# x in two of five raw weight buffers, and eight k tiles through seven products in every second column block of FFN 2

## The chip, the cores and the metric

The kernel runs on one core of one Trainium2 chip. The metric is the time of one execution in microseconds of device time. Engines are named as in the profile: PE (matmul) with PEld (its weight loads), DVE (vector), ACT (scalar), POOL (GpSimd) and SP, whose queue issues most transfers.

## The reference

One encoder layer on x of 256 rows by 2048 columns, in f32. What matters here is the residual x and the two half FFNs:

```python
D_MODEL = 2048
SEQ = 256
D_FF = ((8 * D_MODEL // 3 + 255) // 256) * 256   # 5632

def swiglu(h, w_gate, w_up, w_down):
    return (jax.nn.silu(h @ w_gate) * (h @ w_up)) @ w_down
...
        x = x + 0.5 * swiglu(rms_norm(x, ffn1_norm[i]), ffn1_w_gate[i], ffn1_w_up[i], ffn1_w_down[i])
        h = rms_norm(x, mix_norm[i])
        proj = h @ w_in[i]
...
        x = x + mixed @ w_out[i]
        x = x + 0.5 * swiglu(rms_norm(x, ffn2_norm[i]), ffn2_w_gate[i], ffn2_w_up[i], ffn2_w_down[i])
        gate = jax.nn.sigmoid(rms_norm(x, ple_norm[i]) @ w_ple_gate[i])
...
        x = x + rms_norm(e, ple_post_norm[i])
```

Between the two FFNs stand a state space mixer and a stick-breaking attention, after them a gated embedding.

## The kernel before

Rows are in two tiles of 128 (`TT` = 2), columns in blocks of 512 (`NB`), k in tiles of 128. Every f32 operand of a large product is split into a high part of lower precision (`whi`, `nhi`: a cast on ACT, L168) and the rest (`wlo`, `nlo`: a subtraction on DVE, L171). A product is three matmuls of 128x128 by 512: high by high (L292), low by high (L293), high by low (L297).

Weights come as `raw` tiles of four k tiles by 512 columns (1 MB) through three buffers. A tile is split half by half (two k tiles) into four buffers of `whi` and `wlo`. A plain half is 12 matmuls: 2 k tiles, 2 row tiles, 3 products. FFN 1 and FFN 2 each run 11 column blocks (f = 0 to 10) of gate and up, turn each block's result through `mid` and DMAs into `hT`, and then run four column blocks of down over 44 k tiles.

In FFN 2, from f = 1 on, the first chunk of four k tiles of gate and up goes through seven products instead of eight (`gemm_seven`): with the gate and up tiles cut in halves along k, the weights b11, b21 (gate) and b12, b22 (up) are added on DVE (`sum`, L459: t1 = b11 + b12, t2 = t1 + b22, t4 = t2 + b21, t3 = b12 + b22) and split into `shi` and `slo`; the sums of the rows (`sum_forms`) are made once, while f = 0 runs. A product is 6 matmuls (L452, L453, L455), so the chunk takes 42 where plain halves take 48. The other three chunks of gate follow plainly, then those of up. `opened` and `gated` (L531 to L540) and the lines L545 and L547 close a block by adding the products' accumulators and gating; `turned` transposes it (L203).

The program is written in order and a scheduler lays the instructions out on each engine; `put_off(n, fn)` runs `fn` n steps (`step()`, one after each half or product or two) later. A tile of a pool waits for a free buffer of its tag, in the order of the program. The four `acc` accumulators and two double ones, `aux`, are PSUM.

The residual x stays in its own eight tiles (`xt`, 16 KB in each partition) all through: loaded in FFN 1's block 0 for the sums of squares, added to after down (L594) and after the output projection (L1339).

Of the kernel before, what the change touches and what calls it, by code (L numbers as in the profile page):

```python
# [9 lines left out]
F32 = mybir.dt.float32  # L10
# [6 lines left out]
P = 128  # L17
# [16 lines left out]
def layer_kernel(ctx: ExitStack, tc: tile.TileContext, a: dict, shapes: dict, out: bass.AP):  # L34
# [18 lines left out]
    xpool = ctx.enter_context(tc.tile_pool(name="xres", bufs=1))  # L53
# [86 lines left out]
    xt = [[xpool.tile([P, NB], F32, name=f"x_{t}_{n}") for n in range(ND)] for t in range(TT)]  # L140
# [96 lines left out]
    def first_quarters(w, xn):  # L237

        rest = com("h")
        raws = [wp.tile([P, 4, NB], F32, tag="raw", name=uid("raw"), bufs=3) for _ in range(2)]  # L240
# [37 lines left out]
    def weight_halves(w, k0, nk, n0, own=None):  # L278

        raw = wp.tile([P, 4, NB], F32, tag="raw", name=uid("raw"), bufs=3)  # L280
        src = w[k0 * P : (k0 + nk) * P, n0 : n0 + NB].rearrange("(j p) n -> p j n", p=P)
        nc.sync.dma_start(raw[:, :nk, :], src)
        return weight_split(raw, nk, own)
# [125 lines left out]
    def sum_forms(parts):  # L409
# [9 lines left out]
        for z, (x, y, op) in enumerate((  # L419
            (up[:, :, 1], down[:, :, 1], ALU.subtract), (s[:, 0], up[:, :, 0], ALU.subtract),  # L420
            (up[:, :, 0], up[:, :, 1], ALU.subtract), (down[:, :, 0], s[:, 1], ALU.add),
        )):
            nc.vector.tensor_tensor(out=s[:, z], in0=x, in1=y, op=op)
        both = halves("n")
        split(*both, sums.rearrange("p (z t) -> p z t", z=4))
        return both

    def gemm_seven(act, sums, ws, n0, nkt, pool, first, second):

        raws = []  # L430
        for w in ws:
            raw = wp.tile([P, 4, NB], F32, tag="raw", name=uid("raw"), bufs=3)
            nc.sync.dma_start(raw, w[: 4 * P, n0 : n0 + NB].rearrange("(j p) n -> p j n", p=P))
            raws.append(raw)
        b11, b21, b12, b22 = (raw[:, 2 * h : 2 * h + 2, :] for raw in raws for h in range(2))
        parts = act(0)

        def whole(k, t):
            return [[u[:, 2 * k + j, t * P : (t + 1) * P] for j in range(2)] for u in parts]

        def summed(z):
            return [[u[:, z, j * P : (j + 1) * P] for j in range(2)] for u in sums]

        def product(ps, left, src, own, stop):
            hi, lo = (
                (pool if own else wp).tile([P, 2, NB], F32R, tag=s, name=uid(s), bufs=3 if own else None)
                for s in (("shi", "slo") if own else ("whi", "wlo"))
            )
            split(hi, lo, src)
            lh, ll = left  # L450
            for j in range(2):
                nc.tensor.matmul(ps, lhsT=lh[j], rhs=hi[:, j], start=j == 0, stop=False)  # L452
                nc.tensor.matmul(ps, lhsT=ll[j], rhs=hi[:, j], start=False, stop=False)  # L453
            for j in range(2):
                nc.tensor.matmul(ps, lhsT=lh[j], rhs=lo[:, j], start=False, stop=stop and j == 1)  # L455

        def add(x, y):
            t = pool.tile([P, 2, NB], F32, tag="sum", name=uid("sum"), bufs=2)
            nc.vector.tensor_tensor(out=t, in0=x, in1=y, op=ALU.add)  # L459
# [23 lines left out]
        for w, banks, fresh in ((ws[0], [p2, p4], False), (ws[1], [p38[:, :NB], p38[:, NB:]], True)):  # L483
            for k0 in range(4, nkt, 4):
                part = act(k0 // 4)
                for half in list(weight_halves(w, k0, 4, n0)):
                    begin = k0 == 4 and half[0] == 0
                    end = k0 + 4 >= nkt and half[0] == 1
                    for t in range(TT):
                        gemm_half({t: banks[t]}, (part, half), (t,), fresh and t == 1 and begin, end)  # L490
                    step()
            if not fresh:
                put_off(0, second, p2, p4, p5)
        return p38

    def ffn(i, xn, nxt, bg=None):
# [23 lines left out]
        for f in range(NF):  # L520
# [5 lines left out]
            if sevens and f:  # L526
# [3 lines left out]
                def opened(p1, p67, g=gate_cols, u=up_cols):  # L530
                    nc.scalar.copy(g[0], p1)  # L531
                    nc.vector.tensor_tensor(out=u[0], in0=p67[:, :NB], in1=g[0], op=ALU.add)
                    nc.vector.tensor_tensor(out=u[1], in0=p67[:, NB:], in1=u[0], op=ALU.add)
# [1017 lines left out]
```

## Time and profile before

| | |
|---|---|
| runs | 1870.79, 1872.24, 1873.25 us; median 1872.24 |
| profiled execution | 1872.24 us, span 1870.4 us |
| TensorE clock granted | 1.0 throughout |
| matmuls | 9134 |
| DMA | 400.06 MB, mean 214 GB/s |

The stages, by what their lines do in the trace: FFN 1 gate and up to about 490 us, its down to 737, the mixers to 975, the output projection to 1056, FFN 2 gate and up to 1497, its down to 1737, then the embedding. Busy time in these stretches (us):

| stretch | PE | DVE | ACT | POOL |
|---|---|---|---|---|
| 0 to 490 | 487.85 | 314.56 | 223.46 | 23.23 |
| 490 to 737 | 247.00 | 174.38 | 144.98 | 2.33 |
| 737 to 975 | 234.66 | 162.37 | 150.90 | 19.20 |
| 975 to 1056 | 81.00 | 55.75 | 42.04 | 3.72 |
| 1056 to 1497 | 440.43 | 354.66 | 226.10 | 0.00 |
| 1497 to 1737 | 240.00 | 170.35 | 140.07 | 0.00 |
| 1737 to 1870 | 128.45 | 78.34 | 68.91 | 1.89 |

A busy PE is not a PE at its peak: matmuls are pipelined, so the starts of matmuls, not their lengths, tell the pace.

### The profile page before, as it was taken

The page shows a single profiled execution, that of the slowest core. Times are in us where ns is not written, and L with a number is a line of the kernel's source. Part 1 is how long each engine was busy: PE and PEld are TensorE (multiplying, and loading weights), DVE is VectorE, ACT ScalarE, POOL GpSimd, SP SyncE. Part 2 cuts the span into 40 slices and gives each one's busy share as a digit, 9 for nine tenths or more (in the row PEclk, how much of TensorE's full clock was granted, in tenths as well). Part 3 has the DMA queues.
Part 4 walks back from the last instruction along what each step waited for, and adds up shares of the span by engine and source line. Part 5 has one row for each costly group of instructions (what it writes and reads, how often), then busy time and mean ns, then how long its engine had stood idle before and what let it go on. Part 6 is the DMA issues. An engine that isn't in the chain of part 4 may idle for free.

```text
span 1870.4 us, 23938 instructions
## 1 busy us (share of the span) xinstructions
PE 1859.4 (99%) x9134; PEld 1536.3 (82%) x9134; DVE 1310.4 (70%) x1527; ACT 996.5 (53%) x1151; POOL 50.4 (3%) x84
## 2 busy tenths in 40 slices
PE   9999999999999999999999999999999999999998
PEld 7888888888888888878888888888888888888887
DVE  8867665455576776687567678778787866777655
ACT  7444444444456665456695555445454555666554
POOL 0011000000000000010020000000000000000000
PEclk9999999999999999999999999999999999999999
DMA  8788867766655666675645666575666675656563
GB/s 323 242 278 268 267 208 222 231 217 200 217 196 199 212 199 244 185 248 163 222 147 189 218 205 221 203 220 186 203 205 208 225 228 203 204 202 212 189 224 124
DMA packets 230387, 400.06 MB, mean 214 GB/s; under 512 B 26401, under 2 KB 50337, under 8 KB 229985
## 3 DMA queue, kind: packets, MB, share of 16 engines
q1 hardware_dynamic: 227824, 392.81, 63.7%
q0 software_dynamic: 1728, 4.33, 0.7%
q8 instruction: 71, 1.16, 0.3%
q10 hardware_dynamic: 720, 1.41, 0.2%
q14 instruction: 44, 0.35, 0.1%
HBM read 369.26 MB, written 9.83 MB: 203 GB/s over the span
## 4 chain that ended last, share of the span: by engine, by line
PE 92%; ACT 3%; DVE 2%; DMA 1%; SPq 1%; issue 1%; POOL 0%; DVEq 0%; ACTq 0%; POOLq 0%
PE acc L292 26%; PE acc L297 26%; PE acc L293 26%; PE aux L293 3%; PE aux L292 3%; PE aux L297 3%; ACT whi L168 1%; SPq L1061 1%; PE acc L455 1%; DMA raw<-in_w_in 1%; PE aux L452 1%; PE acc L452 1%; PE acc L453 1%; PE aux L455 1%; PE aux L453 1%
## 5 line engine op out<-in xcount | busy, mean ns | idle before, releaser
L171 DVE TENSOR_TENSOR wlo<-raw,whi 128x1024 fp32r<-128x1024 f32 x656 | 798.2, 1224 | 458.9 <-ACT whi L168 455.3
L168 ACT CAST whi<-raw 128x1024 fp32r<-128x1024 f32 x656 | 686.2, 1053 | 758.7 <-PE acc L293 607.9
L292 PE MATMUL acc<-whi,nhi 128*128 128x512 f32 x1408 | 551.0, 391 | 1.2 <-ACT whi L260 0.5
L293 PE MATMUL acc<-whi,nlo 128*128 128x512 f32 x1408 | 548.2, 389 | 0.0
L297 PE MATMUL acc<-wlo,nhi 128*128 128x512 f32 x1408 | 384.4, 389 | 0.0
L292 PE MATMUL acc<-whi,hhi 128*128 128x512 f32 x816 | 317.6, 389 | 0.0
L293 PE MATMUL acc<-whi,hlo 128*128 128x512 f32 x816 | 317.5, 389 | 0.0
L292 PEld LDWEIGHTS acc<-whi,nhi 128*128 128x128 f32 x1408 | 264.3, 188 | 58.3 <-ACT whi L168 1.7
L297 PEld LDWEIGHTS acc<-wlo,nhi 128*128 128x128 f32 x1408 | 264.2, 188 | 55.6 <-DVE wlo L171 0.4
L293 PEld LDWEIGHTS acc<-whi,nlo 128*128 128x128 f32 x1408 | 264.4, 188 | 54.0
L297 PE MATMUL acc<-wlo,hhi 128*128 128x512 f32 x816 | 221.0, 389 | 0.0
L297 PEld LDWEIGHTS acc<-wlo,hhi 128*128 128x128 f32 x816 | 152.8, 188 | 32.5 <-DVE wlo L171 0.9
L293 PEld LDWEIGHTS acc<-whi,hlo 128*128 128x128 f32 x816 | 153.2, 188 | 32.0
L292 PEld LDWEIGHTS acc<-whi,hhi 128*128 128x128 f32 x816 | 153.1, 188 | 31.8
L171 DVE TENSOR_TENSOR hlo<-hT,hhi 128x1024 fp32r<-128x1024 f32 x88 | 107.1, 1218 | 0.0
L168 ACT CAST hhi<-hT 128x1024 fp32r<-128x1024 f32 x88 | 91.8, 1044 | 0.5 <-PE acc L455 0.4
L292 PE MATMUL aux<-whi,nhi 128*128 128x512 f32 x160 | 62.2, 389 | 0.0
L293 PE MATMUL aux<-whi,nlo 128*128 128x512 f32 x160 | 62.2, 389 | 0.0
L297 PE MATMUL aux<-wlo,nhi 128*128 128x512 f32 x160 | 49.3, 389 | 0.0
L171 DVE TENSOR_TENSOR slo<-sum,shi 128x1024 fp32r<-128x1024 f32 x40 | 48.6, 1214 | 0.4 <-ACT shi L168 0.2
L168 ACT CAST shi<-sum 128x1024 fp32r<-128x1024 f32 x40 | 42.1, 1052 | 11.5 <-DVE sum L459 11.4
L297 PEld LDWEIGHTS aux<-wlo,nhi 128*128 128x128 f32 x160 | 30.0, 188 | 6.2
(312 smaller groups left out, 1314.5 us busy)
## 6 DMA issues: line engine op xcount, KB each, us to landing
raw<-in_ffn_w_up SPq DMA_DIRECT2D x88, 1024.0 KB, 5.9
raw<-in_ffn_w_down SPq DMA_DIRECT2D x88, 1024.0 KB, 5.0
raw<-in_ffn_w_gate SPq DMA_DIRECT2D x86, 1024.0 KB, 5.4
raw<-in_w_in SPq DMA_DIRECT2D x32, 1024.0 KB, 5.5
raw<-in_w_out SPq DMA_DIRECT2D x16, 1024.0 KB, 5.1
raw<-in_w_ple_gate SPq DMA_DIRECT2D x16, 1024.0 KB, 5.1
hT<-mid SPq DMA_DIRECT2D x160, 64.0 KB, 5.0
h<-mid SPq DMA_DIRECT2D x176, 32.0 KB, 3.4
```

The costliest lines, as they stand in the source:

```text
L168: copy = nc.scalar.copy(hi, src)
L171: nc.vector.tensor_tensor(out=lo, in0=src, in1=hi.bitcast(F32), op=ALU.subtract)
L292: nc.tensor.matmul(ps[t], lhsT=lh, rhs=hi[:, j, cols], start=start and j == 0, stop=False)
L293: nc.tensor.matmul(ps[t], lhsT=ll, rhs=hi[:, j, cols], start=False, stop=False)
L297: nc.tensor.matmul(ps[t], lhsT=lh, rhs=lo[:, j, cols], start=False, stop=stop and j == 1)
L452: nc.tensor.matmul(ps, lhsT=lh[j], rhs=hi[:, j], start=j == 0, stop=False)
L453: nc.tensor.matmul(ps, lhsT=ll[j], rhs=hi[:, j], start=False, stop=False)
L455: nc.tensor.matmul(ps, lhsT=lh[j], rhs=lo[:, j], start=False, stop=stop and j == 1)
L1061: nc.sync.dma_start(zt[0][p1 : p1 + HC, z], sv[p0 : p0 + HC, r % 2 * 2 + r // 2])
```

## The change

x gives up its own tiles. The raw weights get five buffers instead of three, and x lives in two of the five: while it is only needed for the sums of squares in FFN 1's block 0, from FFN 1's down to the start of FFN 2, and from FFN 2's down to the end. For the gate and up blocks in between it is given up: before each down stage `fetch_x` loads it again through POOL's queue, in FFN 1 from the input, in FFN 2 from a copy in DRAM (`scr_x`) that is written, also through POOL's queue, as the output projection finishes each column block.

In FFN 2, blocks f = 1, 3, 5, 7, 9 take a second chunk through seven products: chunk 0, then gate's chunks 2 and 3 plainly, then chunk 1 by seven products into the same accumulators, then up's chunks 2 and 3. Even blocks keep one such chunk. The products come in another order (1, 5, 6, 4, 7, 2, 3), and the row sums are made for two chunks, in the `sum` buffers instead of `h`. In the built order PE has 30 matmuls fewer (8610 matmul rows for 8640), DVE 41 instructions more, ACT 16 more, and POOL 24 transfers of 256 KB more.

```diff
-    xpool = ctx.enter_context(tc.tile_pool(name="xres", bufs=1))
...
-    xt = [[xpool.tile([P, NB], F32, name=f"x_{t}_{n}") for n in range(ND)] for t in range(TT)]
+    xt = [[], []]
+
+    def place_x():
+        for t in range(TT):
+            x = wp.tile([P, ND, NB], F32, tag="raw", name=uid("x"), bufs=5)
+            xt[t][:] = [x[:, n, :] for n in range(ND)]
+
+    def fetch_x(rows):
+        place_x()
+        for n in range(ND):
+            for t in range(TT):
+                nc.gpsimd.dma_start(xt[t][n], rows[t * P : (t + 1) * P, n * NB : (n + 1) * NB])
+
+    place_x()
+    scr_x = dramp.tile([T, D], F32, name="scr_x")
...
-        raw = wp.tile([P, 4, NB], F32, tag="raw", name=uid("raw"), bufs=3)
+        raw = wp.tile([P, 4, NB], F32, tag="raw", name=uid("raw"), bufs=5)
...
+    def whole_rows(pool, parts):
 
         hi, lo = parts
-        whole, sums = com("h"), com("h")
-        u = whole.rearrange("p (j t m) -> p j t m", j=4, t=TT)
+        u = pool.tile([P, 2, NB], F32, tag="sum", name=uid("whole"), bufs=2)
         nc.vector.tensor_tensor(
-            out=whole.rearrange("p (j t) -> p j t", j=4), in0=hi.bitcast(F32), in1=lo.bitcast(F32), op=ALU.add
+            out=u.rearrange("p j n -> p (j n)"), in0=hi.bitcast(F32).rearrange("p j t -> p (j t)"),
+            in1=lo.bitcast(F32).rearrange("p j t -> p (j t)"), op=ALU.add,
         )
-        s = sums.rearrange("p (z j m) -> p z j m", z=4, j=2)
-        up, down = u[:, :2], u[:, 2:]
+        return u.rearrange("p j n -> p (j n)").rearrange("p (j x b) -> p j x b", j=4, b=32)
...
+            (a21, a22, ALU.subtract), (s[:, 0], a11, ALU.subtract),
+            (a11, a21, ALU.subtract), (a12, s[:, 1], ALU.add),
...
-        p1, p2 = acc(), acc()
-        product(p1, whole(0, 0), b11, False, True)
-        product(p2, whole(1, 0), b21, False, False)
-        step()
-        t1 = add(b11, b12)
-        p5 = acc()
-        product(p5, summed(0), t1, True, True)
-        t2 = add(t1, b22)
-        p67 = aux()
-        product(p67[:, :NB], summed(1), t2, True, True)
-        step()
-        t4 = add(t2, b21)
-        p4 = acc()
-        product(p4, whole(1, 1), t4, True, False)
-        t3 = add(b12, b22)
-        product(p67[:, NB:], summed(2), t3, True, True)
-        step()
-        p38 = aux()
-        product(p38[:, :NB], summed(3), b22, False, False)
-        step()
-        put_off(0, first, p1, p67)
...
+        def chunk(self, kb, final=()):
+
+            raws = []
+            for w, n0 in self.ws:
+                raw = wp.tile([P, 4, NB], F32, tag="raw", name=uid("raw"), bufs=5)
+                nc.sync.dma_start(
+                    raw, w[4 * kb * P : 4 * (kb + 1) * P, n0 : n0 + NB].rearrange("(j p) n -> p j n", p=P)
+                )
+                raws.append(raw)
+            b11, b21, b12, b22 = (raw[:, 2 * h : 2 * h + 2, :] for raw in raws for h in range(2))
+            parts, sums = self.act(kb), self.sums(kb)
...
+            self.product(1, whole(0, 0), b11, False, final)
+            t1 = self.add(b11, b12)
+            self.product(5, summed(0), t1, True, final)
+            step()
+            t2 = self.add(t1, b22)
+            self.product(6, summed(1), t2, True, final)
+            t4 = self.add(t2, b21)
+            self.product(4, whole(1, 1), t4, True, final)
+            step()
+            t3 = self.add(b12, b22)
+            self.product(7, summed(2), t3, True, final)
+            self.product(2, whole(1, 0), b21, False, final)
+            step()
+            self.product(3, summed(3), b22, False, final)
...
+                s = Seven(xn, lambda kb: sums[kb], ((wg, f * NB), (wu, f * NB)), sevens)
+                if f % 2 == 0:
+                    s.chunk(0, shared)
+                    put_off(0, opened, s)
+                    s.column(0, (1, 2, 3), True)
+                    put_off(0, gated, s)
+                    s.column(1, (1, 2, 3), True)
+                else:
+                    s.chunk(0)
+                    s.column(0, (2, 3))
+                    s.chunk(1, (*shared, 2, 4))
+                    put_off(0, opened, s)
+                    put_off(0, gated, s)
+                    s.column(1, (2, 3), True)
+                nc.vector.tensor_tensor(out=hh, in0=s.banks[3.8], in1=hh, op=ALU.add)
...
-                sums = sum_forms(xn(0))
+                sums = [sum_forms(sevens, whole_rows(sevens, xn(kb))) for kb in range(2)]
...
+        fetch_x(a["x"][0] if bg else scr_x)
...
+            for t in range(TT):
+                nc.gpsimd.dma_start(scr_x[t * P : (t + 1) * P, n * NB : (n + 1) * NB], xt[t][n])
```

DVE, at the start of column block f = 3 (raw_9753 and raw_9755 are its first gate and up tiles, raw_9710 the last up tile of f = 2). Before:

```order
L171 TENSOR_TENSOR wlo_9713<-raw_9710,whi_9712 128x1024
L171 TENSOR_TENSOR wlo_9717<-raw_9710,whi_9716 128x1024
L171 TENSOR_TENSOR wlo_9760<-raw_9753,whi_9759 128x1024
L171 TENSOR_TENSOR wlo_9770<-raw_9753,whi_9769 128x1024
L459 TENSOR_TENSOR sum_9779<-raw_9753,raw_9755 128x1024
L459 TENSOR_TENSOR sum_9792<-sum_9779,raw_9755 128x1024
L171 TENSOR_TENSOR slo_9783<-sum_9779,shi_9782 128x1024
L171 TENSOR_TENSOR wlo_9835<-raw_9755,whi_9834 128x1024
L545 TENSOR_TENSOR h_9428<-aux_9509,h_9428 128x1024
L171 TENSOR_TENSOR slo_9796<-sum_9792,shi_9795 128x1024
L547 SCALAR_TENSOR_TENSOR h_9428<-h_9428,sm_8834,sg_9427 128x512 x2
L459 TENSOR_TENSOR sum_9805<-sum_9792,raw_9753 128x1024
```

And now (raw_9788 and raw_9790 are the gate and up tiles, raw_9745 the last up tile of f = 2):

```order
L184 TENSOR_TENSOR wlo_9748<-raw_9745,whi_9747 128x1024
L487 TENSOR_TENSOR sum_9803<-raw_9788,raw_9790 128x1024
L184 TENSOR_TENSOR wlo_9752<-raw_9745,whi_9751 128x1024
L184 TENSOR_TENSOR slo_9806<-sum_9803,shi_9805 128x1024
L487 TENSOR_TENSOR sum_9816<-sum_9803,raw_9790 128x1024
L184 TENSOR_TENSOR wlo_9793<-raw_9788,whi_9792 128x1024
L487 TENSOR_TENSOR sum_9829<-sum_9816,raw_9788 128x1024
L184 TENSOR_TENSOR slo_9819<-sum_9816,shi_9818 128x1024
L184 TENSOR_TENSOR wlo_9855<-raw_9788,whi_9854 128x1024
L184 TENSOR_TENSOR slo_9832<-sum_9829,shi_9831 128x1024
L487 TENSOR_TENSOR sum_9842<-raw_9790 128x1024
L184 TENSOR_TENSOR wlo_9869<-raw_9790,whi_9868 128x1024
```

The first sums now stand ahead of the last split of the block before, and the add that closes that block (L545, now L601) has moved behind the chunk's third weight split.

DVE, in the middle of the same block. Before, after the first chunk, where gate's second and third tiles (raw_9844 and raw_9881) are split plainly:

```order
L171 TENSOR_TENSOR wlo_9847<-raw_9844,whi_9846 128x1024
L171 TENSOR_TENSOR wlo_9851<-raw_9844,whi_9850 128x1024
L532 TENSOR_TENSOR h_9752<-aux_9794,sg_9751 128x512
L171 TENSOR_TENSOR wlo_9884<-raw_9881,whi_9883 128x1024
L533 TENSOR_TENSOR h_9752<-aux_9794,h_9752 128x512
L171 TENSOR_TENSOR wlo_9888<-raw_9881,whi_9887 128x1024
L171 TENSOR_TENSOR wlo_9918<-raw_9915,whi_9917 128x1024
L171 TENSOR_TENSOR wlo_9922<-raw_9915,whi_9921 128x1024
```

And now the second chunk's products, from the split of t1 (sum_9961) to the split of t3 (sum_9997), with raw_9947 and raw_9949 its gate and up tiles and raw_10029 the next up tile:

```order
L184 TENSOR_TENSOR slo_9964<-sum_9961,shi_9963 128x1024
L487 TENSOR_TENSOR sum_9973<-sum_9961,raw_9949 128x1024
L184 TENSOR_TENSOR wlo_9952<-raw_9947,whi_9951 128x1024
L487 TENSOR_TENSOR sum_9985<-sum_9973,raw_9947 128x1024
L184 TENSOR_TENSOR slo_9976<-sum_9973,shi_9975 128x1024
L184 TENSOR_TENSOR wlo_10010<-raw_9947,whi_10009 128x1024
L184 TENSOR_TENSOR slo_9988<-sum_9985,shi_9987 128x1024
L487 TENSOR_TENSOR sum_9997<-raw_9949 128x1024
L184 TENSOR_TENSOR wlo_10020<-raw_9949,whi_10019 128x1024
L184 TENSOR_TENSOR wlo_10032<-raw_10029,whi_10031 128x1024
L184 TENSOR_TENSOR wlo_10036<-raw_10029,whi_10035 128x1024
L184 TENSOR_TENSOR slo_10000<-sum_9997,shi_9999 128x1024
```

Where plain weight splits stood, sums and splits that depend on one another now stand.

SP's queue, the loads of the same block. Before:

```order
L433 DMA raw_9753<-in_ffn_w_gate 128x4x512
L433 DMA raw_9755<-in_ffn_w_up 128x4x512
L282 DMA raw_9844<-in_ffn_w_gate 128x4x512
L282 DMA raw_9881<-in_ffn_w_gate 128x4x512
L282 DMA raw_9915<-in_ffn_w_gate 128x4x512
L282 DMA raw_9949<-in_ffn_w_up 128x4x512
L282 DMA raw_9988<-in_ffn_w_up 128x4x512
L282 DMA raw_10022<-in_ffn_w_up 128x4x512
```

And now:

```order
L495 DMA raw_9788<-in_ffn_w_gate 128x4x512
L495 DMA raw_9790<-in_ffn_w_up 128x4x512
L295 DMA raw_9879<-in_ffn_w_gate 128x4x512
L295 DMA raw_9913<-in_ffn_w_gate 128x4x512
L495 DMA raw_9947<-in_ffn_w_gate 128x4x512
L495 DMA raw_9949<-in_ffn_w_up 128x4x512
L295 DMA raw_10029<-in_ffn_w_up 128x4x512
L295 DMA raw_10071<-in_ffn_w_up 128x4x512
```

One gate and one up tile of the plain stretch became the pair of the second chunk (the two rows L495 in the middle).

More of the change, by code (lines that the diff above doesn't have):

```diff
@@ L481, in gemm_seven, with whole, summed @@
[L481 to L488 removed]
+        def chunk(self, kb, final=()):
[8 more added lines that the diff above has]
+            parts, sums = self.act(kb), self.sums(kb)
+            def whole(k, t):
+                return [[u[:, 2 * k + j, t * P : (t + 1) * P] for j in range(2)] for u in parts]
+            def summed(z):
+                return [[u[:, z, j * P : (j + 1) * P] for j in range(2)] for u in sums]
+            self.product(1, whole(0, 0), b11, False, final)
[12 more added lines that the diff above has]
+            self.product(3, summed(3), b22, False, final)
+            step()
@@ L489, in gemm_seven, with column @@
+        def column(self, side, kbs, final=False):
+            zs = ((2, 4), (3, 8))[side]
+            w, n0 = self.ws[side]
+            for kb in kbs:
+                part = self.act(kb)
+                for half in list(weight_halves(w, 4 * kb, 4, n0)):
+                    end = final and kb == kbs[-1] and half[0] == 1
                     for t in range(TT):
-                        gemm_half({t: banks[t]}, (part, half), (t,), fresh and t == 1 and begin, end)
+                        ps = self.bank(zs[t])
+                        gemm_half({t: ps}, (part, half), (t,), self.begin(zs[t]), end)
```

80 lines of the change are left out of this document (44 added, 36 removed).

## The prediction

> **What bounds the kernel now.** I read the page's busy shares and chain first, then the TensorE rows of a calm stage, then FFN 2's gate and up stage by its timeline, groups and waits.
>
> ```profile
> PE 1859.4 (99%) x9134; PEld 1536.3 (82%) x9134; DVE 1310.4 (70%) x1527; ACT 996.5 (53%) x1151; POOL 50.4 (3%) x84
> PE 92%; ACT 3%; DVE 2%; DMA 1%; SPq 1%; issue 1%; POOL 0%; DVEq 0%; ACTq 0%; POOLq 0%
> ```
>
> PE is the bound: busy 99% of the span and 92% of the chain. But its mean of 389 ns per matmul is a latency, not a price. The timeline of the first down product gives the price:
>
> ```profile
> 524.89 1.07 PE L297 MATMUL acc<-wlo,hhi 128*128 128x512 f32 x4
> ...
> 527.61 1.07 PE L297 MATMUL acc<-wlo,hhi 128*128 128x512 f32 x4
> ```
>
> One half tile (12 matmuls) takes 527.61 - 524.89 = 2.72 us, so a matmul costs 2.72/12 = 0.2267 us. Next, the starts of five FFN 2 column blocks (f = 1 to 5), each the first matmul of its seven products:
>
> ```profile
> 1097.51 0.39 PE L452 MATMUL acc<-whi,hhi 128*128 128x512 f32 x1
> 1139.79 0.39 PE L452 MATMUL acc<-whi,hhi 128*128 128x512 f32 x1
> 1182.26 0.39 PE L452 MATMUL acc<-whi,hhi 128*128 128x512 f32 x1
> 1225.14 0.39 PE L452 MATMUL acc<-whi,hhi 128*128 128x512 f32 x1
> 1267.49 0.39 PE L452 MATMUL acc<-whi,hhi 128*128 128x512 f32 x1
> ```
>
> A block has 42 + 144 = 186 matmuls, 42.16 us at 0.2267. The blocks took 42.28, 42.47, 42.88 and 42.35: f = 3 loses 0.72 us, f = 4 only 0.19. So the stage runs within 2% of what PE can do, and the loss is in the odd block. Who makes PE wait there (first row), and what held the rest up, stands in the waits of 1066 to 1490 us, the last row being the load queue's:
>
> ```profile
> PEld aux L452 <- ACT shi L168: 2.7, 5, 0.6
> ACT whi L168 <- DMA raw<-in_ffn_w_gate: 20.3, 9, 5.1
> SPq L282 <- DVE sum L459: 138.4, 20, 14.5
> ```
>
> PE waits for the split of a sum; the sum is late because the loads wait (up to 14.5 us) for the DVE to let go of one of three raw buffers.
>
> **The change part by part.** *Fewer matmuls.* A chunk of four k tiles costs 48 matmuls for gate and up plainly, 42 by seven products. The change does a second chunk so in f = 1, 3, 5, 7, 9: 5 x 6 = 30 matmuls fewer, 30 x 0.2267 = 6.80 us, all on the path. [...]
>
> *More work for DVE.* Prices are from the groups of 1066 to 1450 us; the last row is a window, with the busy time of PE, PEld, DVE and ACT:
>
> ```profile
> L171 DVE TENSOR_TENSOR wlo<-raw,whi 128x1024 fp32r<-128x1024 f32 x134 | 162.6, 1221 | 77.2 <-ACT whi L168 76.9
> L171 DVE TENSOR_TENSOR slo<-sum,shi 128x1024 fp32r<-128x1024 f32 x36 | 43.7, 1214 | 0.4 <-ACT shi L168 0.2
> L459 DVE TENSOR_TENSOR sum<-sum,raw 128x1024 f32<-128x1024 f32 x18 | 22.0, 1222 | 0.3
> L203 DVE STREAM_TRANSPOSE mid<-h 128x512 f32<-128x512 f32 x18 | 12.1, 695 | 0.0
> L547 DVE SCALAR_TENSOR_TENSOR h<-h,sm,sg 128x512 f32<-128x512 f32 x16 | 11.3, 745 | 0.0
> L545 DVE TENSOR_TENSOR h<-aux,h 128x1024 f32<-128x1024 f32 x8 | 9.7, 1218 | 0.0
> L537 DVE TENSOR_TENSOR sg<-acc,sg 128x512 f32<-128x512 f32 x8 | 5.5, 684 | 0.0
> L423 DVE TENSOR_TENSOR h<-h,h 128x256 f32<-128x256 f32 x2 | 0.8, 422 | 0.0
> ...
> L168 ACT CAST whi<-raw 128x1024 fp32r<-128x1024 f32 x134 | 139.9, 1052 | 159.3 <-PE acc L293 76.7 <-PE aux L293 40.3 <-DMA raw<-in_ffn_w_gate 18.9
> ...
> 1066.00:1109.00 43.00, 43.00 (x191) 35.51 (x190) 34.54 (x39) 25.00 (x28) 0.00 (x0) 1.00 0.68 230
> ```
>
> Back to back they follow faster than they last (DVE timeline, seven steps from the first to the last row):
>
> ```profile
> 1218.68 1.22 DVE L171 TENSOR_TENSOR wlo<-raw,whi 128x1024 fp32r<-128x1024 f32 x1
> ...
> 1226.63 1.22 DVE L171 TENSOR_TENSOR slo<-sum,shi 128x1024 fp32r<-128x1024 f32 x1
> ```
>
> 7.95/7 = 1.136 us a row of 1024, 0.085 less than it lasts. A chunk needs 3 wlo, 4 slo and 4 sums: 11 x 1.136 = 12.5 us of DVE for 42 x 0.2267 = 9.52 us of PE. Two plain tiles need 4 x 1.136 = 4.5 us for 10.88 us. A block's closing rows (four of 0.69, two of 1.22, two of 0.745, two of 0.695, less 10 x 0.085) take 7.2 us. An odd block then has 30 x 1.136 + 7.2 = 41.3 us of DVE against 180 x 0.2267 = 40.8 of PE, an even one 23 x 1.136 + 7.2 = 33.3 against 42.2. DVE fits the pair (74.6 of 83.0) but must enter each chunk ahead of PE. ACT gains 3 casts of 1.05 us a block and stays near 60%.
>
> Is it ahead? I lay the rows of the DVE order shown with the change end to end, for f = 3, from PE's first product at T. A split waits for one of four whi buffers, free when PE is through the eight high-part matmuls (1.81 us) of the half four earlier. The last up half of f = 2 waits for the half that starts at T - 13.6: high parts done at T - 11.8, cast at T - 10.7, its wlo at T - 9.6; t1 stands just ahead of it, at T - 12.0, its tiles asked for 25 us before T. From T - 9.6 eleven rows of 1.136 (slo 5, t2, wlo, t4, slo 6, wlo, slo 4, t3, wlo, the closing add, wlo), two of 0.66 and slo 7 end at T + 5.4. The add waits only for T + 0.35, the end of the block before. Product 7 is the fifth: PE wants its slo at T + 4 x 1.36 + 4 x 0.227 = T + 6.35. Spare: 1.0 us. In the second chunk (PE from T + 20.4) the last gate split waits likewise for product 3's high parts and ends at T + 11.5; twelve rows on, slo 7 is done at T + 25.2, wanted at 26.75: 1.5 spare. Twenty rows on (15 of 1.136, four of 0.6, two of 0.66) is the next block's slo 7, T + 46.1, wanted at 40.8 + 6.35 = 47.15: 1.0 spare. So nothing stalls, narrowly. In f = 1, t1 stands behind the last up split, so at T - 6.6; twelve rows and the closing ones bring slo 7 at T + 7.35, 1.0 us late: +1.0 once. The second sum form (one row of 1.2, four of 0.42, a split of 1.2: 4.1 us) lies ahead of that, where the window shows DVE with 43 - 34.5 = 8.5 us free.
>
> *Buffers.* With five, each load is asked for when the tile five before it is emptied. For the second chunk of f = 3 these are the last up tile of f = 2, emptied at T - 9.6, and the first chunk's gate tile, at T - 2.8.
>
> ```profile
> raw<-in_ffn_w_up SPq DMA_DIRECT2D x88, 1024.0 KB, 5.9
> x<-in_x SPq DMA_DIRECT2D x8, 256.0 KB, 8.6
> coef<-scr_coef POOLq DMA_DIRECT2D x32, 64.0 KB, 6.6
> POOL sm L1438 <- DVE sq L1431: 871.5, 1, 871.5
> POOL dec L945 <- DVE hlo L171: 441.6, 1, 441.6
> L594 DVE SCALAR_TENSOR_TENSOR x<-acc,x x16: 680/686/693, 550.3 to 1763.2; 128x512 f32<-128x512 f32 x16
> 470.31 23.04 SPq L282 DMA_DIRECT2D raw<-in_ffn_w_down  x5
> 1490.00:1500.00 10.00, 10.00 (x46) 8.27 (x45) 8.07 (x9) 4.15 (x4) 0.00 (x0) 1.00 0.98 296
> ```
>
> At 5.9 us landing the later is there at T + 3.1; t1 of the second chunk wants it at T + 7.7. That also undoes the waits above: of the 0.72 us an odd block loses I keep 0.19 a chunk, the calm block's loss. Terms: four odd blocks 2 x 0.19 - 0.72 = -0.34 each, -1.4; f = 1: 1.0 + 0.38 - 0.12 = +1.3.
>
> *x comes and goes.* Eight loads of 256 KB enter on POOL's queue at each down stage, and eight stores beside the output projection. POOL is idle then (441.6 and 871.5 us in one wait), so nothing queues behind. Down loads begin at 470.3 and x is first used at 550.3; even one after another, two loads of 8.6 us are 17 us, and each later pair has another 264 x 0.2267 = 60 us. They share the DMA engines, full at 296 GB/s (last row): 2.1 MB ahead of all weights would hold these back 7 us, and three raw tiles (5.44 us of PE each, two halves) are 16 us. I take 0; without that cover it is 7 us at each of two places. [...]
>
> Sum: -6.8 - 1.4 + 1.3 = -6.9 us. The profiled execution took 1872.24 us (span 1870.4, 1.84 outside), which is also the median of the three runs, so 1865.3.
>
> **The rivals.** *DVE sets the pace of the second chunk* (slower). If its two tiles land after T + 20, DVE enters it with no lead and PE follows at 12.5 instead of 9.52 us: 5 x 3.0 = 15 us, 1872.2 - 6.9 + 15 = 1880.3. It eats the gain above 1.4 us a block and is slower beyond 2.1. For it: the 20.3 us waited for gate loads. Against: the 4.6 us spare above.
>
> *The narrow places are missed* (no change). If rows follow at 1.22 instead of 1.136, the 32 rows from the second chunk's first slo to the next block's slo 7 slip 2.7 us, 1.7 more than the spare; an estimate of 1.3 us a pair, most of that, gives 5 x 1.3 = 6.5, so 1871.8. Against: 1.136 holds wherever DVE is full.
>
> *Five buffers clear all waits.* No loss at all in odd blocks: 6.8 + 4 x 0.72 + 0.12 = 9.8, so 1862.4 (taking f = 5, 7, 9 as f = 3).
>
> *x hinders the weights* once, 7 us: 1872.3. Against: PE has 16 us in hand.
>
> *The change does not do what it says* is excluded: the built order has 8610 matmul issues against 8640.
>
> **How the numbers follow.** Forecast 0.66, all waits cleared 0.09, narrow places missed 0.12, x hinders 0.03, DVE's pace 0.10. A measurement here can tell about 0.2%, 3.7 us, from no change: the first two are faster (0.75), the next two within it (0.15), the last slower (0.10). The low end is 1862.4 less the 1.45 us by which the fastest run before lies under the median, 1860.9; the high end takes in the missed places with 0.4, 1872.2. Left out is 0.13.
>
> **What would show it.** Right: odd blocks of about 41.2 us and even ones of 42.4 between first products, 180 and 186 matmuls; DVE nearly without idle time in odd blocks; almost no ACT wait for gate loads; no wait for x. Wrong: PE waiting for shi or slo in the second chunk by over 1 us, odd blocks above 42.3 us, or gaps in PE at the start of a down stage.

## The result, and the profile after

The changed kernel takes 1862.13 us (median of four runs, 1861.68 to 1863.78) where the kernel before takes 1872.32 (four runs, 1870.79 to 1873.25): ratio 0.9947, 95% interval 0.9934 to 0.9959. The forecast was 1865.3 us, with a range from 1860.9 to 1872.2. A second measurement (e11_after_again below) gave 1861.93 against 1871.12, ratio 0.9949 (0.9936 to 0.9961).

The profiled execution took 1861.68 us with a span of 1859.6. The page's busy shares and its chain by engine:

```profile
PE 1850.9 (100%) x9104; PEld 1532.3 (82%) x9104; DVE 1349.3 (73%) x1568; ACT 1012.7 (54%) x1167; POOL 63.5 (3%) x108
PE 97%; ACT 2%; DMA 0%; POOL 0%; issue 0%; SPq 0%; POOLq 0%
```

There are 9104 matmul rows where 9134 were, so the thirty are gone; DVE has 41 rows and 39 us more, and the chain that ended last is PE for 97%, where it was 92%. The column blocks, by the timeline of their first matmuls (f = 3 to 6):

```profile
1178.81 0.39 PE L480 MATMUL acc<-whi,hhi 128*128 128x512 f32 x1
...
1219.83 0.39 PE L480 MATMUL acc<-whi,hhi 128*128 128x512 f32 x1
...
1262.11 0.39 PE L480 MATMUL acc<-whi,hhi 128*128 128x512 f32 x1
...
1303.15 0.39 PE L480 MATMUL acc<-whi,hhi 128*128 128x512 f32 x1
```

Odd blocks take 41.02 and 41.04 us, the even one 42.28. The windows of blocks 3 and 4 (length, then the busy time of PE, PEld, DVE, ACT and POOL) show what is left over on DVE:

```profile
1178.81:1219.83 41.02, 41.02 (x181) 33.78 (x180) 40.99 (x41) 24.27 (x26) 0.00 (x0) 1.00 0.61 204
1219.83:1262.11 42.28, 42.28 (x187) 34.91 (x186) 34.39 (x34) 21.55 (x23) 0.00 (x0) 1.00 0.71 226
```

DVE is busy for all but 0.03 us of an odd block, and has 7.9 us free in an even one. The waits of 1056 to 1490 us (time waited, times, longest):

```profile
SPq L295 <- DVE wlo L184: 181.1, 39, 10.1
...
ACT whi L181 <- DMA raw<-in_ffn_w_gate: 5.5, 1, 5.5
...
PEld aux L480 <- ACT shi L181: 0.6, 2, 0.3
```

ACT waits once for a gate tile, for 5.5 us, instead of nine times and 20.3 us; PE's waits for a split sum fall from 2.7 to 0.6 us. The load queue still waits about as long in all (331 us; 346 in the trace of e0 below), now mostly for the splits of tiles: that costs nothing as long as the tile that it asks for is not yet wanted.

### The profile page after: what moved, and what is told of

Its sections match the earlier page's. It is cut to its first block, busy times and chain, and to the rows that moved or that the text cites. A ratio compares the mean times of both kernels' runs of the same rounds, so it can differ in the third digit from the quotient of the medians.

```text
span 1859.6 us, 24021 instructions
## 1 busy us (share of the span) xinstructions
PE 1850.9 (100%) x9104; PEld 1532.3 (82%) x9104; DVE 1349.3 (73%) x1568; ACT 1012.7 (54%) x1167; POOL 63.5 (3%) x108
## 4 chain that ended last, share of the span: by engine, by line
PE 97%; ACT 2%; DMA 0%; POOL 0%; issue 0%; SPq 0%; POOLq 0%
PE acc L305 27%; PE acc L306 27%; PE acc L310 27%; PE aux L305 2%; PE aux L310 2%; PE aux L306 2%; PE acc L480 1%; PE acc L481 1%; PE acc L483 1%; PE aux L480 1%; PE aux L481 1%; PE aux L483 1%; PE aux L1076 0%; ACT whi L181 0%; DMA raw<-in_ffn_w_gate 0%; ACT nhi L191 0%
## 5 line engine op out<-in xcount | busy, mean ns | idle before, releaser
L184 DVE TENSOR_TENSOR wlo<-raw,whi 128x1024 fp32r<-128x1024 f32 x651 | 789.8, 1224 | 410.0 <-ACT whi L181 404.6
L305 PE MATMUL acc<-whi,hhi 128*128 128x512 f32 x776 | 301.9, 389 | 0.0
L306 PE MATMUL acc<-whi,hlo 128*128 128x512 f32 x776 | 301.9, 389 | 0.0
L310 PE MATMUL acc<-wlo,hhi 128*128 128x512 f32 x776 | 209.0, 389 | 0.0
L305 PEld LDWEIGHTS acc<-whi,hhi 128*128 128x128 f32 x776 | 145.6, 188 | 30.3
L310 PEld LDWEIGHTS acc<-wlo,hhi 128*128 128x128 f32 x776 | 145.6, 188 | 30.3
L306 PEld LDWEIGHTS acc<-whi,hlo 128*128 128x128 f32 x776 | 145.6, 188 | 30.2
L181 ACT CAST shi<-sum 128x1024 fp32r<-128x1024 f32 x60 | 63.1, 1052 | 24.0 <-DVE sum L487 21.3
L184 DVE TENSOR_TENSOR slo<-sum,shi 128x1024 fp32r<-128x1024 f32 x60 | 72.7, 1219 | 0.0
L487 DVE TENSOR_TENSOR sum<-sum,raw 128x1024 f32<-128x1024 f32 x30 | 36.6, 1220 | 0.2
```

What stands on the lines that cost most here:

```text
L181: copy = nc.scalar.copy(hi, src)
L184: nc.vector.tensor_tensor(out=lo, in0=src, in1=hi.bitcast(F32), op=ALU.subtract)
L305: nc.tensor.matmul(ps[t], lhsT=lh, rhs=hi[:, j, cols], start=start and j == 0, stop=False)
L306: nc.tensor.matmul(ps[t], lhsT=ll, rhs=hi[:, j, cols], start=False, stop=False)
L310: nc.tensor.matmul(ps[t], lhsT=lh, rhs=lo[:, j, cols], start=False, stop=stop and j == 1)
```

## The experiments

Where the text says "stage", it is FFN 2's gate and up, measured from the first of the seven products' matmuls until down's first result is added to x, so that a delay of PE at the end of gate and up counts too. The expectations of e1, e6, e9 and e10 speak of blocks up to f = 9. There are seven-product blocks up to f = 10: the kernels with two chunks in "every" block have ten such blocks (9074 matmul rows), and the one called six blocks has seven (f = 1, 2, 4, 5, 7, 8, 10; 9092 rows).

### The kernel before again

No edit.

> The kernel before, run again, for its profile. The shift between the two traces is already 2.0 us when FFN 2's first seven-product block begins, and 1.45 us of it is one idle stretch of PE at 822.9 us in the mixer's row PE L959, where both kernels issue the same PE instructions in the same order. Theory A, a chance delay of one execution: the median stays at 1872.3 us, and the stretch is absent or elsewhere in this profile. Theory B, it belongs to the program (how its instructions lie, or what else is in flight): this profile has it again, 1.4 to 1.5 us at the same instruction, and then some 1.5 to 2 of the 10.2 us that the change saved have nothing to do with its seven products.

Measured: 1871.89 us, ratio 1.0001 (0.9992 to 1.001). PE's timeline at the place in question, first in the trace that the prediction was made from:

```profile
820.43 1.02 PE L959 MATMUL aux<-ua,m 64*64 64x64 f32 x51
822.90 0.45 PE L959 MATMUL aux<-ua,m 64*64 64x64 f32 x13 [1.45 <-issue]
```

and in this execution:

```profile
820.74 1.16 PE L959 MATMUL aux<-ua,m 64*64 64x64 f32 x64
```

The idle stretch is gone, as theory A has it: it is not in every execution of the program. Beside the first four experiments the kernel before ran 27 times, 16 times in 1870.08 to 1871.60 us and 11 times in 1872.27 to 1873.16. The forecast's base of 1872.24 us lies 1.2 us above the median of these 27 (1871.06), and the 1872.32 of the first comparison 1.3 us: about 1 of its 10.2 us is the base and not the change. The second comparison gives 9.2. Against this second trace (span 1868.7) the changed kernel's is shorter by 9.1 us; 0.3 us of shift stand before the stage and 8.9 us arise in it.

The blocks of this trace are those to compare with. The first matmuls of f = 3, 4 and 5:

```profile
1180.54 0.39 PE L452 MATMUL acc<-whi,hhi 128*128 128x512 f32 x1
...
1223.46 0.39 PE L452 MATMUL acc<-whi,hhi 128*128 128x512 f32 x1
...
1265.81 0.39 PE L452 MATMUL acc<-whi,hhi 128*128 128x512 f32 x1
```

An odd block took 42.92 us (42.90 to 42.92 for f = 3, 5, 7, 9), an even one 42.35.

### Five buffers, one chunk

```diff
-                if f % 2 == 0:
+                if True:
                     s.chunk(0, shared)
...
-                sums = [sum_forms(sevens, whole_rows(sevens, xn(kb))) for kb in range(2)]
+                sums = [sum_forms(sevens, whole_rows(sevens, xn(kb))) for kb in range(1)]
```

> The changed kernel with one chunk of seven products in every block f from 1 to 9, so with before's count of 9134 matmul rows: x moved, five raw buffers, the new order inside a chunk, and no second chunk. Theory: the ten or so stalls of PE behind late raw tiles leave (odd blocks 42.88 to about 42.3 us, so 5 x 0.55 = 2.7 us), and the 30 matmuls stay: 1869.5 us, ratio 0.9985, ACT no longer waits for gate loads. If the 1.5 to 2 us ahead of FFN 2 come with the moved x, 1867.7, ratio 0.9975. Rival, the buffers are most of the gain and the matmuls are hidden: 1864 or less, ratio 0.9955.

Measured: 1867.41 us (1867.12 to 1868.17 in 11 runs), ratio 0.9978 (0.9969 to 0.9986). First matmuls of f = 2, 3 and 4:

```profile
1137.70 0.39 PE L480 MATMUL acc<-whi,hhi 128*128 128x512 f32 x1
...
1179.98 0.39 PE L480 MATMUL acc<-whi,hhi 128*128 128x512 f32 x1
...
1222.26 0.39 PE L480 MATMUL acc<-whi,hhi 128*128 128x512 f32 x1
```

All nine blocks from f = 1 to 9 take 42.28 us, 380.5 together, against 383.5 in the trace of e0: five buffers with the new order of products take 3.0 us out of the stage (which of the two does it was not taken apart), and no stall of the odd blocks is left. The kernel is 3.65 us faster than the one before (medians), where the theory had 2.7 from the odd blocks. The rest of the change's gain, 5.9 us of the stage from this trace to that of the changed kernel, is the second chunk's.

### Two chunks, three buffers

The changed kernel with x back in tiles of its own, `fetch_x` and `scr_x` left out:

```diff
-        raw = wp.tile([P, 4, NB], F32, tag="raw", name=uid("raw"), bufs=5)
+        raw = wp.tile([P, 4, NB], F32, tag="raw", name=uid("raw"), bufs=3)
...
-    place_x()
+    xt[:] = [[xpool.tile([P, NB], F32, name=f"x_{t}_{n}") for n in range(ND)] for t in range(TT)]
```

> The second chunk alone: x stays in its own tiles and is never moved, the raw tag keeps three buffers, and odd blocks take two chunks (9104 matmul rows). Theory, the buffers are what lets VectorE run ahead: the second chunk's two raw tiles can only be asked for when the first chunk's are free, its first sum begins some microseconds after PE is ready, PE then goes at VectorE's pace, and each of five odd blocks loses 1 to 3 us against the changed kernel: 1867 to 1877 us, likeliest 1870, ratio 0.999, with 'PEld <- DVE or ACT' waits in the second chunk. Rival, the buffers do not matter and the 30 matmuls are all there is: 1862 to 1865.5, ratio 0.996.

Measured: 1890.1 us, ratio 1.0099 (1.0085 to 1.0113). The thirty matmuls are gone here too, and the kernel is 19 us slower than before. Without the buffers the second chunk is a loss. But it is not lost where the theory put it. PE's timeline in f = 3, whose first product is at 1179.74:

```profile
1182.36 0.73 PE L472 MATMUL acc<-slo,nhi 128*128 128x512 f32 x2 [0.15 <-DVE slo L173]
1185.89 0.80 PE L469 MATMUL aux<-shi,nhi 128*128 128x512 f32 x1 [2.81 <-ACT shi L170]
...
1188.19 0.63 PE L470 MATMUL aux<-whi,nlo 128*128 128x512 f32 x1
1188.62 0.63 PE L469 MATMUL aux<-whi,nhi 128*128 128x512 f32 x1
...
1191.98 0.39 PE L469 MATMUL acc<-whi,hhi 128*128 128x512 f32 x1
1192.21 0.40 PE L470 MATMUL acc<-whi,hlo 128*128 128x512 f32 x1
```

The wait of 2.81 us is in the block's first chunk, at product 6; f = 5, 7 and 9 have one of 2.80 us each. DVE's timeline says why t2, which product 6 needs, came late:

```profile
1176.28 1.22 DVE L476 TENSOR_TENSOR sum<-raw,raw 128x1024 f32<-128x1024 f32 x1
...
1179.94 1.23 DVE L590 TENSOR_TENSOR h<-aux,h 128x1024 f32<-128x1024 f32 x1 [0.86 <-PE aux L299]
1181.08 1.22 DVE L173 TENSOR_TENSOR slo<-sum,shi 128x1024 fp32r<-128x1024 f32 x1
1182.21 1.41 DVE L592 SCALAR_TENSOR_TENSOR h<-h,sm,sg 128x512 f32<-128x512 f32 x2
1183.54 1.22 DVE L476 TENSOR_TENSOR sum<-sum,raw 128x1024 f32<-128x1024 f32 x1
```

t1 begins 3.5 us ahead of the first product (1176.28), where the changed kernel has 11.6 us. So late, the closing rows of the block before (L590, L592), which can only run once PE has ended that block, stand ahead of t2; from the first of them to t2 it is 3.6 us. Then there is a second price: after the wait matmuls follow 0.43 us apart (1188.19, 1188.62) instead of 0.23, until 1191.98. The windows show the granted clock (the number after the five engines' busy times):

```profile
1182.00:1184.00 2.00, 0.93 (x3) 0.30 (x2) 2.00 (x4) 0.00 (x0) 0.00 (x0) 1.00 0.00 0
...
1188.00:1190.00 2.00, 2.00 (x6) 1.52 (x6) 2.00 (x3) 0.00 (x0) 0.00 (x0) 0.50 0.96 300
```

It is 1.00 before and 0.50 after the wait; from 1185.89 to 1191.98 these are 14 matmuls, at 0.43 instead of 0.227 us another 2.8 us. From its first product to that of its second chunk, f = 3 takes 26.88 us here and 20.50 in the changed kernel; the second chunk with its up tiles takes 20.55 (20.52 in the changed kernel) and lost nothing. The same holds in f = 5, 7 and 9, whose first parts lose 5.2 to 6.4 us, and the even blocks from f = 4 on lose some 1.2 to 1.3 us each.

### The transfers of x alone

The kernel before, x in its own tiles, with the 24 transfers:

```diff
...
+        fetch_x(a["x"][0] if bg else scr_x)
...
         if side:
+            for t in range(TT):
+                nc.gpsimd.dma_start(scr_x[t * P : (t + 1) * P, n * NB : (n + 1) * NB], xt[t][n])
```

> The kernel before with the 24 transfers of x alone: x keeps its tiles, is reloaded from its input after FFN 1's last gate and up block, stored to scratch when the mixer has summed it and reloaded after FFN 2's last block, all on GpSimd's queue; three raw buffers, one chunk a block. Theory: the transfers hide behind 60 us of down projection each time: 1872.3 us, ratio 1.000 within 0.001. Rival, a reload ends late or holds a raw or weight transfer back: 7 us at one or both places, 1879 to 1886, ratio 1.004 to 1.0075.

Measured: 1871.95 us, ratio 1.0002 (0.9993 to 1.0011): nothing. The DMA view of the changed kernel has the same transfers (KB each, median us to landing):

```profile
x<-in_x POOLq DMA_DIRECT2D x8, 256.0 KB, 5.3
scr_x<-x POOLq DMA_DIRECT2D x8, 256.0 KB, 2.6
x<-scr_x POOLq DMA_DIRECT2D x8, 256.0 KB, 7.3
```

### More work for DVE in the second chunk

One addition more, and three:

```diff
             t3 = self.add(b12, b22)
+            if kb == 1:
+                for _ in range(1):      # 3 in the other
+                    nc.vector.tensor_tensor(out=t3, in0=b12, in1=b22, op=ALU.add)
```

> The changed kernel with one addition issued once more (b12 + b22 into the same tile, 1.14 us a step on VectorE) in the second chunk of the five odd blocks. Theory, the second chunk is narrow: in the trace slo 7 of the second chunk ends at T + 26.7 us where PE wants it at T + 26.75, so hardly 0.2 us is spare, PE waits about 1 us more in each odd block, and the even block with 34 of 42.3 us busy takes nothing over: 5 x 1.0 = 5 us, 1867 us, ratio to before 0.9972, which is no gain over the five buffers alone. Rival, the spare is the 1.5 us of the prediction: 1862 to 1863, ratio 0.9947.

> The same addition issued three times more, 3.4 us a second chunk. Theory: 5 x (3.4 - 0.1) = 16 us, 1878 us, ratio 1.003, slower than before; from the first to the second of these kernels 2.27 us an odd block, the full price. Rival, VectorE runs ahead in the even blocks and some of it hides: 1868 to 1873.

Measured: 1867.21 us, ratio 0.998 (0.9971 to 0.9988), and 1877.47 us, ratio 1.0033 (1.002 to 1.0045). Both numbers came, but not in the way that the expectations give. The first took the end of the second chunk's slo 7 for its start and added a row to it; in truth 1.4 us are spare there (next section). PE's stop of e4 in f = 6 is not in a second chunk but in the even block after it, at product 4:

```profile
1312.29 0.50 PE L480 MATMUL acc<-shi,hhi 128*128 128x512 f32 x1 [0.93 <-ACT shi L181]
```

and DVE's rows ahead of it, in that block's first 8 us (first product at 1306.14):

```profile
1308.62 1.41 DVE L606 SCALAR_TENSOR_TENSOR h<-h,sm,sg 128x512 f32<-128x512 f32 x2
1309.94 1.22 DVE L487 TENSOR_TENSOR sum<-sum,raw 128x1024 f32<-128x1024 f32 x1
1311.08 0.71 DVE L216 STREAM_TRANSPOSE mid<-h 128x512 f32<-128x512 f32 x1
1311.71 1.18 DVE L487 TENSOR_TENSOR sum<-raw 128x1024 f32<-128x1024 f32 x1
```

With one row of 1.14 us more, the scheduler laid t4 and t3 of f = 6 behind the closing rows, as it laid t2 in e2; in the changed kernel both stand ahead of them. So e4 changes the order as well as the work, and its 5 us are not the price of the work alone. Against the changed kernel the pairs from f = 1, 3, 5 and 7 on lost 0, 0.2, 2.3 and 1.3 us: a lead seems to be used up first. (Of the 2.3, f = 5 itself loses 1.0, 0.7 of it ahead of its second chunk.) From one to three additions the price is 10.3 us for ten rows, 1.03 a row of 1.14, nearly the full price that the second expectation names. But in e5 too PE does not stop in the second chunk: from f = 5 on the odd blocks lose 2.0 us ahead of it (22.5 us instead of 20.5 from first product to second chunk) and the even ones from f = 4 on 1.7 to 2.4, and the order of e5 differs again from that of e4. So a row's price at a fixed order was not measured.

### Two chunks in every block

```diff
-                if f % 2 == 0:
+                if False:
```

> The changed kernel with two chunks in every block f from 1 to 9, so 24 matmuls fewer than the changed one (9080 rows). By PE alone: 4 x 1.24 = 5.0 us less, 1857.1, ratio 0.992. Theory: VectorE is busy 41.0 of an odd block's 41.0 us and its rows add up to 41.3, and there is no even block any more in which it gets ahead, so a block takes 41.3 to 41.6 us: 9 x 41.3 = 372 against the 374 us of 5 x 41.04 + 4 x 42.28, 1859.5 us, with PE waiting for VectorE's sums or low parts in every block; up to 1864 where the order inside a block adds 0.5 us of its own.

Measured: 1863.54 us, ratio 0.9959 (0.9945 to 0.9972); the time lies in the forecast's range, at its slow end. The theory's 41.3 to 41.6 us a block are hardly a gain over the pairs of 41.02 and 42.28 (mean 41.65), and there is none. f = 1 and 2 take 41.04 us each, f = 3 and 4 41.33 and 41.27, and then it is 42.3 to 43.0 in most. One of the stops, in f = 6:

```profile
1310.15 0.50 PE L480 MATMUL acc<-shi,hhi 128*128 128x512 f32 x1 [1.62 <-ACT shi L181]
```

### The same, with t3 on GpSimd

```diff
-            t3 = self.add(b12, b22)
+            t3 = b12
+            nc.gpsimd.tensor_tensor(out=t3, in0=b12, in1=b22, op=ALU.add)
```

> The same as the kernel with two chunks in every block, and t3 = b12 + b22 is made by GpSimd, in place over b12, which takes 1.14 us of 20.6 off VectorE in each chunk. Theory: VectorE then has 39.0 us of work in a block of 40.9 us, GpSimd's addition (its 128x256 rows take 1.0 to 1.14 us in the mixer, so 4 to 4.6 us at four times the size) has the 10 us from t1 to product 7, and PE sets the pace: 1857 us, ratio 0.992. Rival, GpSimd's addition comes too late or slows VectorE's rows beside it: each of 18 costs 1 to 3 us, 1875 to 1910 us.

Measured: 1887.81 us, ratio 1.0089 (1.0075 to 1.0103): the rival. GpSimd's and DVE's timelines at one such addition:

```profile
1202.51 3.18 POOL L518 TENSOR_TENSOR raw<-raw 128x1024 f32<-128x1024 f32 x1 [17.50 <-DVE sum L487]
...
1202.21 1.23 DVE L184 TENSOR_TENSOR wlo<-raw,whi 128x1024 fp32r<-128x1024 f32 x1
1203.34 3.43 DVE L487 TENSOR_TENSOR sum<-sum,raw 128x1024 f32<-128x1024 f32 x1
```

The DVE row that begins while GpSimd's runs takes 3.43 us instead of 1.22, and ends 1.08 us after GpSimd's (1205.69 to 1206.77), about its own length. It lasted 2.2 us longer. So a chunk loses 2.2 us of DVE to save 1.14.

Two chunks at 1.07 us would make a full DVE 2.1 us slower in each block; against the kernel before it, f = 3 to 9 take 1.9 us more on average. f = 2 takes nothing more, but f = 1 takes 8.4 us more, a third of the 24.3 us between the two kernels. There the second chunk's up tile landed late (DVE waited 1.65 us for it), a split beside GpSimd's addition lasted 2.1 us longer than the usual 1.22, and PE waited long:

```profile
1128.62 1.22 PE L483 MATMUL aux<-slo,nhi 128*128 128x512 f32 x2 [4.86 <-DVE slo L184]
```

In the course of that wait the granted clock fell to 0.50, for 6.8 us; the mean clock over 1095 to 1495 us is 0.99.

### Four buffers

The changed kernel with `bufs=4` for every `raw` tile, x in two of the four.

> The changed kernel with four raw buffers where it has five (x still moved). With three, each odd block lost 3 to 6 us. Theory, the second chunk's loads are what counts: with four they are asked for when the first chunk's two tiles come free, some 6 and 8 us after its first product, so they land 11 to 14 us after it where the five had them there at 3, the first sum of the second chunk comes 3 to 6 us later than at T + 8.4, and an odd block loses 2 to 4 us: 1872 to 1882 us, no gain left. Rival, four are enough and one of x's two tiles would have done: 1862 to 1864.

Measured: 1887.29 us, ratio 1.0085 (1.0071 to 1.0098), slower than the theory's range. In the stage 15.3 us are lost against the changed kernel, 3.4 a pair of blocks, near the forecast. But they are not lost in the second chunk, where the theory put them. In f = 3 that chunk's t1 does begin 8.0 us later after the first product than in the changed kernel (T + 16.4), and yet the block loses only 0.3 us from there on and 2.0 us ahead of it. As in e2, t1 of the first chunk comes only 3.5 us ahead of the first product, the closing rows stand ahead of t4, and PE waits at product 4; the even blocks f = 2, 4 and 8 lose 1.9 to 2.0 us as well. PE's largest wait of 1095 to 1495 us:

```profile
PE acc L480 <- ACT shi L181: 11.5, 7, 1.7
```

Another 9.3 us are lost ahead of the stage, 4.9 of them by 807 us and the rest mostly by 916, which the expectation had left out: while x holds two of four, two are left for the weights there, where before had three and the change has three too. ACT waits 50.9 us there for the mixer's weights (`raw<-in_w_in`), where the changed kernel has 13.4. A wait of PE of 2.23 us, up to 812.02, is followed by 3.4 us at a granted clock of 0.50 (the number after the five engines' busy times):

```profile
812.02 0.50 PE L305 MATMUL acc<-whi,nhi 128*128 128x512 f32 x1 [2.23 <-ACT whi L181]
...
813.00:816.40 3.40, 3.00 (x7) 1.83 (x7) 3.40 (x4) 1.81 (x2) 0.00 (x0) 0.50 0.08 33
```

### A later end of the block, in ten and in seven blocks

The changed kernel again, as the comparison on the same chip:

> The changed kernel again, so that the three beside it are compared on one chip: 1862.1 us, ratio 0.9947; its odd blocks 41.0 us and its even ones 42.28 between first products, as in its first profile.

Measured: 1861.93 us (1861.54 to 1862.11), ratio 0.9949, with blocks of 41.02 and 42.28 us as before.

The two others have `if False:` (ten blocks) and `if f % 3 == 0:` (seven) for `if f % 2 == 0:`, and in both:

```diff
-                nc.vector.tensor_tensor(out=hh, in0=s.banks[3.8], in1=hh, op=ALU.add)
...
-                put_off(2, turned, hp, f, hh)
+                if f < NF - 1:
+                    put_off(2, closed, s)      # the three closing rows, as a function
+                    put_off(3, turned, hp, f, hh)
...
```

> Two chunks in every block f from 1 to 9, and the three VectorE rows that close a block (the last sum with up's banks and the two products with the gate, 2.6 us) issued two steps later, so that the order puts the next block's t4 ahead of the products and t3 ahead of the second. In the kernel with two chunks in every block, PE lost 0.3 us in the third and fourth block and 1.3 to 2.2 in most of the later ones, waiting for ACT's shi behind such a sum. Theory, order: 1.4 to 2.1 us of each of these waits go, and VectorE's 41.3 us a block is what is left: 1858.5 to 1861 us, ratio 0.993. Rival, VectorE is full and any order only moves the wait to another row: 1863.5 us as before, ratio 0.996.

> The same later end, and two chunks in six blocks (f = 1, 2, 4, 5, 7, 8) where the change has five, so 6 matmuls less than the changed kernel. Theory: two such blocks in a row went at PE's pace in the kernel with all nine (41.04 and 41.04 us), and a block with one chunk, in which VectorE has 34 us of work in 42, gives it back what it lost: 1862.1 - 1.2 = 1860.9 us, ratio 0.994. Rival, the second of the two blocks loses 0.3 to 2 us each time: 1861.5 to 1866.

Measured: 1860.6 us (1860.4 to 1861.3), ratio 0.9943 (0.993 to 0.9955), with ten blocks of two chunks; 1861.0 (1860.55 to 1862.03), ratio 0.9944 (0.9931 to 0.9958), with seven. So order was about half of what e6 lost: moving three rows brings 2.9 us, and the blocks f = 1 to 9, which lay 7.9 us above nine times 41.04 in e6, lie 4.1 above it now. The kernel with ten blocks is the fastest of these, 1.3 us under the changed one, and their runs do not overlap. The one with seven came out at the 1860.9 of its theory, but with seven blocks and not six, so 12 matmuls less than the changed kernel (2.7 us) and not 6: f = 2 keeps PE's pace, f = 5 and 7 lose 0.4 to 0.5 us each. Its runs overlap with the changed kernel's. What is left in the kernel with ten is DVE. Windows of f = 1 and f = 6:

```profile
1095.50:1136.50 41.00, 41.00 (x181) 33.75 (x180) 40.97 (x40) 24.14 (x26) 0.00 (x0) 1.00 0.61 208
...
1301.80:1343.60 41.80, 41.48 (x182) 33.69 (x182) 41.46 (x41) 24.45 (x27) 0.00 (x0) 1.00 0.69 226
```

The later blocks take 41.7 to 41.8 us with DVE nearly full (41.46 of 41.80) and PE waiting. That is no less than the mean of the changed kernel's pairs, (41.02 + 42.28)/2 = 41.65; the gain comes from the first four blocks, while DVE still has a lead.

## Why the prediction was right, and where its terms were off

**The thirty matmuls.** Forecast -6.80 us. Each odd block fell from 42.28 (e1) to 41.02, 1.25 us where 6 x 0.2267 is 1.36; five are 6.2. The stages of e1 and the changed kernel are 5.9 us apart, with 0.3 us given back in f = 8 and f = 10. The price holds, less 0.1 us a block for the second chunk.

**The stalls.** This is the term that was mis-sized: forecast -1.4 + 1.3 = -0.1 us; e1 shows -3.0, and in the changed kernel itself, whose blocks f = 1 to 9 are 9.0 us shorter than in e0, -2.2 are left beside the 6.8 for the matmuls. Three steps of it failed. The one that weighs most is f = 1. The prediction put its t1 at T - 6.6, behind the last up split, and so slo 7 1.0 us late. DVE's timeline of the changed kernel, where T is 1095.49:

```profile
1086.18 1.22 DVE L487 TENSOR_TENSOR sum<-raw,raw 128x1024 f32<-128x1024 f32 x1
...
1099.12 1.23 DVE L184 TENSOR_TENSOR slo<-sum,shi 128x1024 fp32r<-128x1024 f32 x1
```

t1 begins at T - 9.3 and slo 7 ends at T + 4.9: 1.5 us in hand, no stall, and f = 1 takes 41.04 us like the others. Then, of an odd block's loss 2 x 0.19 us were kept, while 0.22 stayed (41.02 against 40.80). And the even blocks, taken as unchanged, went from 42.35 (f = 2: 42.48) to 42.28. The rival "five buffers clear all waits", given 0.09, was nearer to what happened: its 1862.4 is within 0.3 us of the median. It came that near in part by luck, with a base that was itself 1.2 us high by the later medians; on the base of 1871.06 it would say 1861.3, and the forecast 1864.1.

**DVE's walk through f = 3.** Four of its points, then the two matmul rows of PE that want slo 7, with T = 1178.81:

```profile
1167.23 1.22 DVE L487 TENSOR_TENSOR sum<-raw,raw 128x1024 f32<-128x1024 f32 x1
...
1183.78 1.22 DVE L184 TENSOR_TENSOR slo<-sum,shi 128x1024 fp32r<-128x1024 f32 x1
...
1187.23 1.22 DVE L487 TENSOR_TENSOR sum<-raw,raw 128x1024 f32<-128x1024 f32 x1
...
1203.13 1.22 DVE L184 TENSOR_TENSOR slo<-sum,shi 128x1024 fp32r<-128x1024 f32 x1
...
1185.23 0.62 PE L483 MATMUL aux<-slo,nhi 128*128 128x512 f32 x2
...
1205.73 0.62 PE L483 MATMUL aux<-slo,nhi 128*128 128x512 f32 x2
```

t1 at T - 11.6 (forecast -12.0); slo 7 done at T + 6.2 (5.4) and wanted at 6.4, so 0.2 us are spare and not 1.0; t1 of the second chunk at T + 8.4 (7.7); its slo 7 done at T + 25.5 (25.2) and wanted at 26.9, 1.4 spare (1.5). The walk, made from the order and row prices alone, was right within 0.8 us, which is most of the 1.0 us that it counted as spare in the first chunk. That nothing stalls, but narrowly, fits with e4, where one row more, with the other order that it brought, costs 5 us.

**The transfers of x.** Forecast 0; e3 shows 0 within 0.1%, and the page after no wait of PE for x.

**The rival "DVE's pace in the second chunk".** It does not happen with five buffers. With three (e2) the kernel does turn slower, and by more than the rival's 1880.3; but the stop is in the block's first chunk, where a late t1 leaves the closing rows ahead of t2 and the granted clock then falls to 0.50 for 6.8 or 3.4 us; the prediction had neither. e2 also has the new order of products, which asks for t2 one product earlier than before did; its part in the 19 us was not taken apart.

**"Narrow places missed"** was put at 1.3 us a pair, and with one row more and another order (e4) two later pairs lost 2.3 and 1.3. In the change itself they were not missed.

## What to carry to other kernels

Ask of a change that shifts work to a second engine not whether the engine fits on average, but whether it enters each step with a lead and which buffers give it that lead: here the kernel with thirty matmuls less is 9.2 us faster than the one before with five raw buffers, and 19 us slower with three. When the second engine is nearly full, look at rows in its queue that wait for the first engine's end of a block: put behind the next block's urgent rows, three of them were worth 2.9 us (e9 against e6). And take the base from many runs: a median of three stood 1.2 us above that of 27 later ones.

## What the runs showed that was not expected

- Beside the wait of 4.86 us in e7, five waits of PE of 2.23 to 2.81 us were followed by a lower granted clock: it stood at 0.50 for 6.8 us (e2, f = 3 and 7) or 3.4 us (f = 5 and 9) after the four of 2.80 and 2.81 us, and for 3.4 us after the one of 2.23 us in e8's mixer. Shorter waits left it at 1.00: the one of 1.76 us in the changed kernel up to 972.09 (windows of 970 to 976 us), and the one of 1.62 us in e6 up to 1310.15 (window of 1302.9 to 1345.8 us). The row of 1182 to 1184 us in e2 shows the clock still at 1.00 in the wait's first microsecond.
- A 128x1024 f32 addition took GpSimd 2.9 to 3.4 us beside a full DVE (e7, 11 of them in 1178 to 1400 us). DVE's sums and splits of these 222 us lasted up to 3.43 us where their medians are 1.22, in all 22 us longer than at the medians, 2.0 for each addition.
- The kernel before ran in two groups of times beside the first experiments, about 1.9 us apart by their medians; of its 38 other runs eight lie between the two. In one trace (1872.24 us) PE stands idle for 1.45 us in the mixer; in one of e3, the same kernel with the transfers of x (1872.99 us), f = 1 takes 44.04 us, since DVE waits 2.0 us there for an up tile. Whether each run of the upper group has a delay of this kind was not settled. Five buffers with one chunk (e1) ran 11 times within 1.05 us.
